# Softmax over 4096 rows: narrow loads of 512 columns in the first tile, and loops that begin at the second tile

## Chip, cores and metric

The kernel runs on one core of a Trainium2 chip. The metric is the device time of one execution in microseconds (us). Runs of the kernel before took 2485.54, 2485.56 and 2485.92 us; the median is 2485.56.

## What is computed

A softmax with a temperature over the last axis of 16 x 256 x 32768 float32 numbers:

```python
scaled = logits / temperature          # temperature = 1.0
scaled = scaled - scaled.max(axis=-1, keepdims=True)
exp_scaled = np.exp(scaled)
return exp_scaled / exp_scaled.sum(axis=-1, keepdims=True)
```

The input has 537 MB and the output as much. Each number is read from memory once and written once.

## The kernel before

A row of 32768 numbers is cut into two halves of 16384, and each half lies on one partition. A tile is 128 such halves, that is 64 rows, so there are 64 tiles (`G`), each 8.4 MB. The array `X` in on-chip memory has three slots (`_BUFS`) of one tile each; tile g uses slot g mod 3. A tile is loaded into its slot, worked on in place, and stored from there.

All transfers are issued by SyncE (SP), in an order written out by `order` (L93) and carried out at L296: loads of tiles 0, 1, 2, store 0, load 3, stores 1 and 2, then load i and store i - 1 by turns, and at the end loads 62 and 63 and stores 61, 62, 63. Each is one instruction with a row of 64 KB per partition, with these exceptions (`load_parts` L68, `store_parts` L76):

- Tile 0's load is one wide load of the first 15360 columns (L151), and then the last 1024 columns (`_NARROW`) in 19 narrow loads (L149). Each narrow load takes 2 to 14 rows that lie 9 apart; the groups come from `narrow_rows` (L82), largest first. Together they cover the 128 rows once.
- Tile 3's load and tile 0's store are in two halves, and the last store is in three parts.

Ahead of a load SP waits until the slot's last store has landed (L144), and ahead of a store until VectorE and ScalarE have scaled the tile (L159, L163).

VectorE and ScalarE work on one tile after another, in pieces of 6304, 5376 and 4704 columns (six pieces in the last two tiles). VectorE waits for the load (`landed`, L198) and takes each piece's negated maximum (L215). ScalarE turns each piece into exponentials and their sum (L275). VectorE swaps the sums and maxima between the two halves of a row (L233) and works out the factors (L237 to L260, with a small exponential on ScalarE, L286). At last VectorE scales two pieces (L266) and ScalarE the first (L294). Neither touches the order of the transfers: they only raise the semaphores that SP waits for.

The instructions of VectorE and ScalarE are written out for the first four tiles (`_HEAD`) and the last three (`_TAIL`); the 57 tiles between are a loop of 19 turns with three tiles each (L307). In the loop the awaited semaphore values are registers that count the turns; a looped tile raises one semaphore per engine and slot when it is scaled, in place of one per piece (L192). `landed` waits for a part of a load ahead of the first piece that needs it: in tile 0 piece 2 alone needs the narrow loads, in tile 3 piece 0 needs the first half, piece 1 both.

At the end SP waits for all stores (L301).

Of the kernel before, what the change touches and what calls it, by code (L numbers as in the profile page):

```python
# [9 lines left out]
_BUFS = 3  # L10
_PLAIN = ((6304, 5376, 4704), (0,))
_LATE = ((4096, 3072, 3072, 2048, 2048, 2048), (3, 4, 5))
_LAST_STORES = ((0, 4096), (4096, 6144), (10240, 6144))
_NARROW = 1024
_NARROW_ROWS = (
    (13, 2), (12, 3), (14,), (11, 3), (10, 4), (9, 5), (8, 6), (7, 7), (4, 4, 3, 3),
)
_HEAD = 4
_TAIL = 3


# [46 lines left out]
def load_parts(g):  # L68
    if g == 0:
        return [(0, _W - _NARROW), (_W - _NARROW, _NARROW)]  # L70
    if g == 3:
        return [(0, _W // 2), (_W // 2, _W // 2)]
    return [(0, _W)]


def store_parts(g, n):  # L76
    if g == 0:
        return [(0, _W // 2), (_W // 2, _W // 2)]
    return list(_LAST_STORES) if g == n - 1 else [(0, _W)]


def narrow_rows(p):  # L82
    step = len(_NARROW_ROWS)
    rows = []
    for q, counts in enumerate(_NARROW_ROWS):
        for n in counts:
            rows.append(slice(q, q + (n - 1) * step + 1, step))
            q += n * step
    assert sum(map(sum, _NARROW_ROWS)) == p
    return sorted(rows, key=lambda r: r.start - r.stop)  # L90


def order(n):  # L93
    plan = [("L", 0), ("L", 1), ("L", 2), ("S", 0), ("L", 3), ("S", 1), ("S", 2)]
    for i in range(4, n - 2):
        plan += [("L", i), ("S", i - 1)]
    return plan + [("L", n - 2), ("L", n - 1), ("S", n - 3), ("S", n - 2), ("S", n - 1)]


@with_exitstack  # L100
def kernel(
# [6 lines left out]
    nc = tc.nc  # L108
    inv_t = 1.0 / float(temperature)
    P = nc.NUM_PARTITIONS  # L110
# [8 lines left out]
    x = xf.rearrange("n (h v) -> (n h) v", h=2)  # L119
    o = of.rearrange("n (h v) -> (n h) v", h=2)  # L120
    G = N * 2 // P
# [6 lines left out]
    X = nc.alloc_sbuf_tensor("xs", [P, _BUFS * _W], fp32)  # L128
# [2 lines left out]
    J = [nc.alloc_sbuf_tensor(f"junk{q}", [P, 2 * most], fp32) for q in range(_BUFS)]  # L131
    R = [nc.alloc_sbuf_tensor(f"row{q}", [P, 4], fp32) for q in range(_BUFS)]
    sig = Signals(nc)
    stored = {}

    def load(g):
        p = Place(g, G)
        rows = slice(g * P, (g + 1) * P)
        for j, (s, n) in enumerate(load_parts(g)):
            if g >= _BUFS:  # L140
                parts = store_parts(g - _BUFS, G)
                for i, (a, m) in enumerate(parts):
                    if a < s + n and s < a + m:
                        nc.sync.wait_ge(*stored[g - _BUFS][i])  # L144
            where = slice(p.slot * _W + s, p.slot * _W + s + n)
            key = ("ld", j, *p.key)
            if g == 0 and j == 1:
                for some in narrow_rows(P):
                    sig.dma(key, nc.sync.dma_start(out=X[some, where], in_=x[some, s : s + n]))  # L149
            else:  # L150
                sig.dma(key, nc.sync.dma_start(out=X[:, where], in_=x[rows, s : s + n]))  # L151

    def store(g):
        p = Place(g, G)
        rows = slice(g * P, (g + 1) * P)
        stored[g] = []
        for i, (s, n) in enumerate(store_parts(g, G)):
            if p.looped:
                nc.sync.wait_ge(sig[("scaled", *p.key)], 2 * p.n)  # L159
            else:  # L160
                for group in (p.own, p.on_act):
                    for k in [k for k in group if k in p.over(s, n)][-1:]:
                        nc.sync.wait_ge(sig[("scaled", k, *p.key)], p.n)  # L163
            where = slice(p.slot * _W + s, p.slot * _W + s + n)
            stored[g].append(
                sig.dma(
                    ("st", i, p.slot),
                    nc.sync.dma_start(out=o[rows, s : s + n], in_=X[:, where]),  # L168
                )
            )  # L170

    class Work:

# [24 lines left out]
        def landed(self, engine, k, seen):  # L198
            s, n = self.p.pieces[k]
            for j, (a, m) in enumerate(load_parts(self.p.g)):  # L200
                if a < s + n and s < a + m and j not in seen:
                    seen.add(j)
                    times = len(narrow_rows(P)) if self.p.g == 0 and j == 1 else 1
                    value = self.p.n16
                    if self.p.g == 3 and j == 1:
                        value, times = 16 * len(narrow_rows(P)) + 16, 1
                    engine.wait_ge(sig[("ld", j, *self.p.key)], value * times)

        def vector(self):
            t, e, r, tv, f, K = self.t, self.e, self.r, self.tv, self.j, self.K  # L210
# [82 lines left out]
                xs = self.piece(k)  # L293
                self.scaled(a.mul(out=xs, in_=xs, mul=f[:, k : k + 1]), k, self.p.on_act)  # L294

    for what, g in order(G):  # L296
        if what == "L":
            load(g)
        else:
            store(g)  # L300
    for key in [key for key in sig.made if key[0] == "st"]:  # L301
        nc.sync.wait_ge(sig[key], sig.made[key])

    for engine, part in ((nc.vector, Work.vector), (nc.scalar, Work.scalar)):
        for g in range(_HEAD):
            part(Work(Place(g, G)))
        with engine.Fori(1, 1 + turns) as turn:  # L307
            turn16 = engine.snap(turn * 16) if engine is nc.vector else None
            for j in range(_BUFS):
                part(Work(Place(_HEAD + j, G, turn, turn16)))  # L310
        for g in range(G - _TAIL, G):
            part(Work(Place(g, G)))

# [34 lines left out]
```

## Time and profile before

| what | value |
|---|---|
| median of the runs | 2485.56 us |
| the profiled execution | 2485.45 us |
| its span, first to last instruction | 2483.7 us |
| moved by DMA, mean rate | 1073.78 MB, 432 GB/s |
| median time from issue to landing, loads / stores of a whole tile | 48.0 / 29.1 us |
| idle time of VectorE that ended with a load's landing | 617.4 us in 60 waits |
| idle time of ScalarE that ended with a maximum (L215) | 1045.6 us in 64 waits |

The chain that ended last, by share of the span: DMA 61%, VectorE 28%, ScalarE 7%.

The page divides the span into 40 slices. A digit is the busy share of a slice in tenths. The chain of waits is followed back from the last instruction, at each step to what released it. A tile passes through the DMA engines about every 38.6 us, load and store together: the loads of successive looped tiles release VectorE at 200.60, 239.69 and 278.77 us at first, and at 2366.22 and 2404.92 us at the end. The trace also keeps every DMA packet with its start, its duration and its size, 17024 of them with data. A row of a transfer is one packet; each transfer ends with semaphore writes of 4 bytes, which the page counts as packets under 512 B (2240).

### The profile page before, as it was taken

The page shows a single profiled execution, that of the slowest core. Times are in us where ns is not written, and L with a number is a line of the kernel's source. Part 1 is how long each engine was busy: PE and PEld are TensorE (multiplying, and loading weights), DVE is VectorE, ACT ScalarE, POOL GpSimd, SP SyncE. Part 2 cuts the span into 40 slices and gives each one's busy share as a digit, 9 for nine tenths or more (in the row PEclk, how much of TensorE's full clock was granted, in tenths as well). Part 3 has the DMA queues.
Part 4 walks back from the last instruction along what each step waited for, and adds up shares of the span by engine and source line. Part 5 has one row for each costly group of instructions (what it writes and reads, how often), then busy time and mean ns, then how long its engine had stood idle before and what let it go on. Part 6 is the DMA issues. An engine that isn't in the chain of part 4 may idle for free.

```text
span 2483.7 us, 1689 instructions
## 1 busy us (share of the span) xinstructions
DVE 1526.0 (61%) x776; ACT 1325.6 (53%) x529; POOL 0.2 (0%) x4
## 2 busy tenths in 40 slices
DVE  5845665666656656566565665656656666566665
ACT  4744645646546455464554645546455464554654
POOL 0000000000000000000000000000000000000000
DMA  9999999999999999999999999999999999999998
GB/s 409 432 437 431 432 437 434 434 433 437 433 432 437 434 434 434 435 434 433 436 434 434 434 435 435 433 435 435 432 435 435 436 432 435 436 432 435 435 436 387
DMA packets 19267, 1073.78 MB, mean 432 GB/s; under 512 B 2240, under 2 KB 2240, under 8 KB 2368
## 3 DMA queue, kind: packets, MB, share of 16 engines
q1 hardware_dynamic: 19264, 1073.75, 99.9%
q14 instruction: 3, 0.02, 0.0%
HBM read 536.87 MB, written 536.87 MB: 432 GB/s over the span
## 4 chain that ended last, share of the span: by engine, by line
DMA 61%; DVE 28%; ACT 7%; issue 2%; SPq 0%; DVEq 0%
DMA xs<-in_logits_dram 59%; DVE t L215 21%; ACT xs L275 6%; DVE xs L266 6%; DMA out_dram<-xs 3%; SPq L168 0%; ACT ee L286 0%; DVE junk L260 0%; DVE t L233 0%; DVE row L257 0%; ACT xs L294 0%; DVE row L237 0%; DVE junk L244 0%; DVEq L307 0%; DVEq L231 0%
## 5 line engine op out<-in xcount | busy, mean ns | idle before, releaser
L275 ACT ACTIVATE xs<-xs,t 128x6304 f32<-128x6304 f32 (+5 forms) x198 | 932.0, 4707 | 1052.5 <-DVE t L215 1045.6
L215 DVE TENSOR_REDUCE t<-xs 128x1 f32<-128x6304 f32 (+5 forms) x198 | 1110.0, 5662 | 617.4 <-DMA xs<-in_logits_dram 617.4
L294 ACT ACTIVATE xs<-xs,junk 128x6304 f32<-128x6304 f32 (+1 forms) x68 | 355.6, 5235 | 44.9 <-DVE junk L260 44.9
L266 DVE TENSOR_SCALAR xs<-xs,junk 128x5376 f32<-128x5376 f32 (+2 forms) x130 | 358.7, 2802 | 2.3
L233 DVE LOAD_MASK_SELECT t<-t x64 | 0.9, 14 | 282.8 <-ACT xs L275 282.8
L286 ACT ACTIVATE ee<-t,row 128x6 f32<-128x6 f32 (+1 forms) x64 | 19.2, 300 | 35.2 <-DVE row L237 35.2
L275 ACT ACTIVATION_READ_ACCUMULATOR xs<-xs,t 128x1 f32 x198 | 36.9, 186 | 0.0
L244 DVE CUSTOM_DVE_ANT_1 junk<-ee,t 128x6 f32<-128x6 f32 (+1 forms) x64 | 10.7, 166 | 23.5 <-ACT ee L286 23.5
L260 DVE TENSOR_SCALAR junk<-ee,row 128x3 f32<-128x3 f32 (+1 forms) x64 | 14.6, 228 | 2.2
L257 DVE RECIPROCAL row<-row 128x1 f32<-128x1 f32 x64 | 10.5, 163 | 2.2
L237 DVE TENSOR_REDUCE row<-t 128x1 f32<-128x6 f32 (+1 forms) x64 | 10.2, 159 | 2.2
L233 DVE STREAM_SHUFFLE t<-t 128x6 f32<-128x6 f32 (+1 forms) x64 | 10.4, 163 | 0.5
L244 DVE DVE_READ_ACCUMULATOR2_ANT row<- 128x1 f32 x64 | 5.3, 82 | 0.0
L275 ACT ACT_TABLE_LOAD x1 | 1.3, 1283 | 0.9 <-SPq L127 0.9
L329 POOL MEMSET const-bfloat16-1.0<- 128x1 bf16 x1 | 0.1, 101 | 0.0
L329 POOL MEMSET const-uint8-127<- 128x1 uint8 x1 | 0.1, 101 | 0.0
L329 POOL MEMSET const-float32-0.0<- 128x1 f32 x1 | 0.1, 98 | 0.2 <-issue 0.2
L329 POOL MEMSET const-float32-1.0<- 128x1 f32 x1 | 0.1, 98 | 0.0
## 6 DMA issues: line engine op xcount, KB each, us to landing
out_dram<-xs SPq DMA_DIRECT2D x2, 4096.0 KB, 28.0
xs<-in_logits_dram SPq DMA_DIRECT2D x2, 4096.0 KB, 19.3
xs<-in_logits_dram SPq DMA_DIRECT2D x1, 7680.0 KB, 21.1
out_dram<-xs SPq DMA_DIRECT2D x2, 3072.0 KB, 19.4
out_dram<-xs SPq DMA_DIRECT2D x1, 2048.0 KB, 12.2
xs<-in_logits_dram SPq DMA_DIRECT2D x62, 48.0
out_dram<-xs SPq DMA_DIRECT2D x62, 29.1
xs<-in_logits_dram SPq DMA_DIRECT2D x4, 12.0 KB
```

What stands on the lines that cost most here:

```text
L215: m = v.tensor_reduce(out=t[:, k : k + 1], in_=self.piece(k), axis=mybir.AxisListType.X, op=A.max, negate=True,)
L233: v.stream_shuffle(out=t[:, 2 * K : 4 * K], in_=t[:, 0 : 2 * K], mask=swap), "sh"
L237: v.tensor_reduce(out=r[:, 0:1], in_=tv[:, :, 0, :], axis=mybir.AxisListType.XY, op=A.min),
L244: v.tensor_tensor_reduce(out=f[:, 0 : 2 * K].rearrange("p (a k) -> p a k", a=2), in0=self.ev, in1=tv[:, :, 1, :], scale=1.0, scalar=0.0, o ...
L257: self.done(v.reciprocal(out=r[:, 2:3], in_=r[:, 1:2]), "rc")
L260: v.tensor_scalar_mul(out=f[:, 0:K], in0=e[:, 0:K], scalar1=r[:, 2:3]), "f"
L266: v.tensor_scalar_mul(out=xs, in0=xs, scalar1=f[:, k : k + 1]), k, self.p.own
L275: s = a.activation(out=xs, in_=xs, func=Exp, bias=t[:, k : k + 1], scale=inv_t, accum_out=t[:, K + k : K + k + 1],)
L286: a.activation(out=self.ev, in_=self.tv[:, :, 0, :], func=Exp, bias=r[:, 0:1], scale=-1.0),
L294: self.scaled(a.mul(out=xs, in_=xs, mul=f[:, k : k + 1]), k, self.p.on_act)
L329: nc = _bacc.Bacc("TRN2", target_bir_lowering=False, num_devices=1)
```

## The change

Two constants change: the narrow loads take the last 512 columns of tile 0 and the wide load the first 15872, with the same 19 groups of rows; and the instructions of VectorE and ScalarE are written out for tile 0 alone, after which a loop of 20 turns covers tiles 1 to 60. The rest of the diff makes the semaphores fit the loop: the parts of a load share one semaphore (the narrow loads have their own), and VectorE waits for the whole load of a tile ahead of its first piece, in tile 3 for both halves; tile 0 keeps its two waits. For that each turn has two counted register values in place of one. The list `order` is replaced by loops that issue the same transfers in the same order. At the end SP waits for 16 instead of 32 on the semaphore that the second part of the last store shares with that of tile 0's.

The diff, without the part that spells out the order and the tuple of SP's store:

```diff
-_NARROW = 1024
+_NARROW = 512
...
-_HEAD = 4
+_HEAD = 1
...
+def stored(g, n):
+    parts = len(store_parts(g, n))
+    return [(("st", i, g % _BUFS), 16 * (g // _BUFS + 1 if i == 0 else 1)) for i in range(parts)]
...
             if g >= _BUFS:
-                parts = store_parts(g - _BUFS, G)
-                for i, (a, m) in enumerate(parts):
+                parts = zip(store_parts(g - _BUFS, G), stored(g - _BUFS, G))
+                for (a, m), (which, value) in parts:
                     if a < s + n and s < a + m:
-                        nc.sync.wait_ge(*stored[g - _BUFS][i])
+                        nc.sync.wait_ge(sig[which], value)
             where = slice(p.slot * _W + s, p.slot * _W + s + n)
-            key = ("ld", j, *p.key)
             if g == 0 and j == 1:
                 for some in narrow_rows(P):
-                    sig.dma(key, nc.sync.dma_start(out=X[some, where], in_=x[some, s : s + n]))
+                    sig.dma(
+                        ("narrow",), nc.sync.dma_start(out=X[some, where], in_=x[some, s : s + n])
+                    )
             else:
-                sig.dma(key, nc.sync.dma_start(out=X[:, where], in_=x[rows, s : s + n]))
+                sig.dma(
+                    ("ld", *p.key), nc.sync.dma_start(out=X[:, where], in_=x[rows, s : s + n])
+                )
...
             for j, (a, m) in enumerate(load_parts(self.p.g)):
-                if a < s + n and s < a + m and j not in seen:
+                if self.p.g == 0 and a < s + n and s < a + m and j not in seen:
                     seen.add(j)
-                    times = len(narrow_rows(P)) if self.p.g == 0 and j == 1 else 1
-                    value = self.p.n16
-                    if self.p.g == 3 and j == 1:
-                        value, times = 16 * len(narrow_rows(P)) + 16, 1
-                    engine.wait_ge(sig[("ld", j, *self.p.key)], value * times)
+                    if j == 0:
+                        engine.wait_ge(sig[("ld", *self.p.key)], 16)
+                    else:
+                        engine.wait_ge(sig[("narrow",)], 16 * len(narrow_rows(P)))
+            if self.p.g > 0 and k == 0:
+                engine.wait_ge(sig[("ld", *self.p.key)], self.p.n16)
...
         for g in range(_HEAD):
             part(Work(Place(g, G)))
         with engine.Fori(1, 1 + turns) as turn:
-            turn16 = engine.snap(turn * 16) if engine is nc.vector else None
+            count16 = [None, None]
+            if engine is nc.vector:
+                count16 = [engine.snap((turn + k) * 16) for k in range(2)]
             for j in range(_BUFS):
-                part(Work(Place(_HEAD + j, G, turn, turn16)))
+                g = _HEAD + j
+                part(Work(Place(g, G, turn, count16[g // _BUFS])))
```

More of the change, by code (lines that the diff above doesn't have):

```diff
@@ L90, in narrow_rows @@
     return sorted(rows, key=lambda r: r.start - r.stop)
[L93 to L97, printed above, removed]
+def stored(g, n):
+    parts = len(store_parts(g, n))
+    return [(("st", i, g % _BUFS), 16 * (g // _BUFS + 1 if i == 0 else 1)) for i in range(parts)]
 @with_exitstack
@@ L133, with load @@
     sig = Signals(nc)
-    stored = {}
-    def load(g):
-        p = Place(g, G)
+    def load(p):
+        g = p.g
         rows = slice(g * P, (g + 1) * P)
@@ L140, in load, with store @@
             if g >= _BUFS:
-                parts = store_parts(g - _BUFS, G)
-                for i, (a, m) in enumerate(parts):
+                parts = zip(store_parts(g - _BUFS, G), stored(g - _BUFS, G))
+                for (a, m), (which, value) in parts:
                     if a < s + n and s < a + m:
-                        nc.sync.wait_ge(*stored[g - _BUFS][i])
+                        nc.sync.wait_ge(sig[which], value)
             where = slice(p.slot * _W + s, p.slot * _W + s + n)
-            key = ("ld", j, *p.key)
             if g == 0 and j == 1:
                 for some in narrow_rows(P):
-                    sig.dma(key, nc.sync.dma_start(out=X[some, where], in_=x[some, s : s + n]))
-            else:
-                sig.dma(key, nc.sync.dma_start(out=X[:, where], in_=x[rows, s : s + n]))
-    def store(g):
-        p = Place(g, G)
+                    sig.dma(
+                        ("narrow",), nc.sync.dma_start(out=X[some, where], in_=x[some, s : s + n])
+                    )
+            else:
+                sig.dma(
+                    ("ld", *p.key), nc.sync.dma_start(out=X[:, where], in_=x[rows, s : s + n])
+                )
+    def store(p):
+        g = p.g
         rows = slice(g * P, (g + 1) * P)
-        stored[g] = []
         for i, (s, n) in enumerate(store_parts(g, G)):
@@ L164, in store @@
             where = slice(p.slot * _W + s, p.slot * _W + s + n)
[L165 to L170, printed above, removed]
+            sig.dma(("st", i, p.slot), nc.sync.dma_start(out=o[rows, s : s + n], in_=X[:, where]))
     class Work:
@@ L294, in scalar @@
                 self.scaled(a.mul(out=xs, in_=xs, mul=f[:, k : k + 1]), k, self.p.on_act)
[L296 to L302, printed above, removed]
+    for g in range(_BUFS):
+        load(Place(g, G))
+    store(Place(0, G))
+    load(Place(_BUFS, G))
+    for g in (1, 2):
+        store(Place(g, G))
+    for g in range(_BUFS + 1, G):
+        load(Place(g, G))
+        if g < G - 2:
+            store(Place(g - 1, G))
+    for g in range(G - _TAIL, G):
+        store(Place(g, G))
+    counts = {}
+    for g in range(G):
+        for which, value in stored(g, G):
+            counts[which] = value
+    for which, value in counts.items():
+        nc.sync.wait_ge(sig[which], value)
     for engine, part in ((nc.vector, Work.vector), (nc.scalar, Work.scalar)):
```

## The prediction

> **What bounds the kernel now.** I read first the page's slices and its list of DMA queues, then the busy time by windows, then the chain of waits, and last the single DMA packets that the trace keeps.
>
> ```profile
> DVE 1526.0 (61%) x776; ACT 1325.6 (53%) x529; POOL 0.2 (0%) x4
> ...
> DMA  9999999999999999999999999999999999999998
> ...
> q1 hardware_dynamic: 19264, 1073.75, 99.9%
> ```
>
> The 16 DMA engines are busy in every slice; the compute engines are not. Now the windows (columns: stretch, its length, busy us of DVE, ACT and POOL, clock, DMA share, GB/s):
>
> ```profile
> 1.50:4.50 3.00, 0.00 (x0) 0.69 (x1) 0.00 (x0) 1.00 0.99 328
> 4.50:20.50 16.00, 0.00 (x0) 0.00 (x0) 0.00 (x0) 1.00 1.00 430
> 20.50:28.00 7.50, 5.90 (x1) 0.00 (x0) 0.00 (x0) 1.00 1.12 393
> ...
> 140.00:300.00 160.00, 88.85 (x39) 76.36 (x29) 0.00 (x0) 1.00 1.00 432
> 300.00:2400.00 2100.00, 1293.77 (x657) 1122.21 (x436) 0.00 (x0) 1.00 1.00 434
> ...
> 2476.00:2484.00 8.00, 0.00 (x0) 0.00 (x0) 0.00 (x0) 1.00 0.25 108
> ```
>
> The reader is to see three losses against 434 GB/s: the first packets, the stretch 20.5 to 28 us in which the narrow loads run, and the last 8 us, in which only some engines still work.
>
> The packets explain these. On one DMA engine the next packet starts 3 to 4 ns before the last one's recorded end, so all packets can be strung into 16 chains. From tile 1 on the chains have no hole but three of 302 ns (at 187.5, 268.4 and 931.9 us). A packet of 65536 B takes 2418 ns (median; 32768 B takes 1213, 16384 B 611), and a chain moves one tile in 8 of them. So an engine's end is the sum of its own packets, and the kernel ends with the slowest engine. The narrow loads put an unequal number of rows on the engines: the chains show 0 to 19 narrow packets, 8 on average. Five chains (us from the first instruction; the last column is the last packet of tile 1's load):
>
> ```
> narrow packets  wide load ends  tile 1 begins  its first packet, ns  tile 1 ends
>       0             21.21          21.21              3434              41.97
>       5             21.16          22.05              3733              42.70
>      11             21.01          23.28              3313              43.52
>      14             21.34          24.56              2840              44.32
>      19             20.91          25.17              2616              44.72
> ```
>
> Sixteen engines finish tile 1 spread over 2.76 us, and the last store spread over 5.16 us: the last packet ends at 2481.96, the first engine's last at 2476.80. The engine that ends last is not one with 19 narrow packets. It is one that finished tile 1 at 43.52 us, 1.55 us behind the first engine, with 11 of them, and that then falls back some 20 ns in each of the 130 DMAs that follow (about 2.4 us), plus 0.08 and 0.37 us in disturbed packets around 158 and 235 us and 0.75 us at 932 us, where one 302 ns hole and a packet of 2835 ns fall on it. The others end at 2480.8 or before.
>
> **The change part by part.** All sums are for that last engine, against the profiled execution's own 2485.45 us (span 2483.7, 1.75 around it), which is 0.11 below the median of 2485.56.
>
> *Wide load, 15360 to 15872 columns:* its 8 packets grow by 2048 B each. Between 61440 B (2267 ns) and 65536 B (2418 ns) a byte costs 0.0369 ns, so 75.5 ns a packet: **+0.60 us** on all engines alike.
>
> *Narrow loads, 4096 to 2048 B a packet:* no packet of 2048 B with data is in the trace. The nearest row, 4096 B, takes 159 ns undisturbed and 287 at most; the slope above gives 84 undisturbed. On the engine of interest 11 of them with their semaphore writes took 23.28 - 21.01 = 2.27 us, 207 ns each. Lower end: undisturbed, 88 ns each with the write, 0.97 us. Upper end: the price does not fall at all, 2.27 us. I take the same disturbance in proportion, 207 x 84/159 = 109 ns, 1.20 us: **-1.07 us** (0 to -1.30).
>
> *The disturbance of tile 1:* its first packet took 3313 ns on this engine, 895 over 2418, while the other engines still read narrow rows. That phase gets half as long, so I take half, **-0.45 us** (0 to -0.90).
>
> *Issue of the narrow loads:* still 19 instructions, and they are covered:
>
> ```profile
> 1.38 13.88 SPq L149 DMA_DIRECT2D xs<-in_logits_dram  x19
> 15.31 0.89 SPq L151 DMA_DIRECT2D xs<-in_logits_dram  x2
> 22.10 17.34 DVE L215 TENSOR_REDUCE t<-xs 128x1 f32<-128x6304 f32 x3 [22.10 <-DMA xs<-in_logits_dram]
> ```
>
> SP has issued tile 2's load at 16.2 us, 4.7 us before the first engine ends the wide load (20.89). The third row starts 0.60 us later, and with it tile 0's store (50.84). That is hidden: the first engine has tiles 1 and 2 to load until 61.3 us.
>
> *Tile 3's merged wait:* VectorE waited for the halves of tile 3's load separately and now waits for both ahead of the first piece. Behind that wait stand tile 3's reductions, then ScalarE's exponentials and SP's store. Both halves are in at 102.8 us by the packets and VectorE reaches tile 3 at 107.96 after tile 2, so it costs nothing; without these 5.1 us of cover it could cost the 9.7 us between the halves.
>
> *Loop from tile 1:* three tiles' code goes from VectorE and ScalarE, one more turn comes:
>
> ```profile
> L307 DVEq FUSED_REGOPS  x19: 44/44/44, 131.1 to 2235.2; - x19
> L307 DVEq ALU_OP  x19: 40/40/52, 263.0 to 2350.8; - x19
> L307 DVEq COMPARE_BRANCH  x19: 50/56/69, 263.0 to 2350.9; - x19
> ```
>
> A turn costs VectorE 0.14 us, and one register operation more, perhaps 0.2. At tile 1 VectorE has no idle time to hide it in, but tile 1's store waits until 84.35 us behind tile 3's second load, while its data are ready at 79.3; and tile 2's store, issued at 108.4, has engines with work until 119.4. Cost nothing; a stall would have to pass 11 us to leave an engine dry. SP's list of transfers and its order stay; a looped tile's store waits on one semaphore's total in place of two pieces' own, for the same instructions. The dropped final wait for the second part of the last store lies ahead of the third part on each engine: nothing.
>
> *The holes:* 302 ns is what 8192 B take at the rate above, and code goes; whether a hole leaves the last engine I can't tell: 0 to -0.75, I take 0, since the 932 us hole falls where VectorE and ScalarE repeat their loop.
>
> Sum: 0.60 - 1.07 - 0.45 = **-0.9 us**, 2484.5 against this execution, 2484.6 against the median. The engines with 19 packets gain 0.60 - 2.0 - 0.1 = -1.5 and stay behind it in rank.
>
> **Rivals.** *Flat packets:* a narrow packet's price in this crowd may be per packet and not per byte (246 ns at the 75th percentile against 159). Then narrow loads keep their 2.27 us and the wide load's 0.60 is added: 2486.1. The Trainium skill, "DMA: Bandwidth & Descriptors", section Bandwidth, says that transfers under 64 KB are dominated by their descriptors, which leans this way; the undisturbed 159 ns, in line with 1213 and 2418, do not.
>
> *Re-spread:* disturbed packets at 158 and 235 us cost this engine 0.45 us; they depend on how the phases fall and could give the gain back: about 2485.4.
>
> *Luck:* the 932 us hole falls on another engine, or the disturbed packets stay away: another 0.45 to 0.75 less, about 2484.0 to 2483.4.
>
> *Phases too close (slower):* the engines would leave tile 1 spread over about 1.4 us in place of 2.76. If closeness made them meet in memory at each tile, the stretch at 140 to 300 us shows the price: 432 in place of 434 GB/s over 2100 us is 9.7 us, 2494. The Trainium skill, same page, section Latency and other measured facts, tells of rows a large power of two apart that halve the rate, and suspects streams in lock-step. It speaks against this change; rows here lie 64 KiB apart. Against it: in the wide load all engines run within 0.62 us of each other, and their packets settle at the floor of 2267 ns after the first one's 2959 (mean). It decides only where the spread falls below these 0.62 us, or for loads beside stores, which no row shows that close.
>
> *Stall at the loop (slower):* over 11 us at tile 1 or 2, each us more being one us: 2486 and up. At the later turns up to 10 us of it would be hidden under VectorE's wait for loads, so the trace does not exclude it. The Trainium skill, "Runtime: NRT & Kernel Launch", section Instruction fetch mechanics, says that a taken branch out of the window stalls for a fetch; no row shows one of this size.
>
> **How the numbers follow.** Forecast (2484.1 to 2485.1) 0.51; re-spread 0.18; luck 0.13; flat packets 0.11; phases 0.05; stall 0.01; something over 5 us faster 0.01. Two in a thousand of this kernel is 5.0 us, about what a measurement can tell from no change; all but the last three cases lie within it: faster 0.01, same 0.93, slower 0.06. The range goes from luck with the lower ends, 2483.2, to flat packets with half a us of disturbed ones, 2486.6.
>
> **What would show it.** Narrow packets of 84 to 150 ns; the engine with 11 ending tile 1 near 42.6 us; the spread after tile 1 under 2 us; packets of 2418 ns from 300 us on; the last 8 us moving more than 108 GB/s. A hole in a chain before 300 us, or 65536 B packets with a median over 2422 ns, would prove me wrong.

## The result, and the profile after

The changed kernel took 2503.84 us in the median of 20 runs (2485.57 to 2510.36); the kernel before 2485.9 (2485.08 to 2486.27, 20 runs). The ratio is 1.0052, with a 95% interval of 1.0036 to 1.0067: it is slower. The forecast was 2484.6 us, with a range of 2483.2 to 2486.6.

The times of the changed kernel form two groups: 8 of the 20 between 2485.6 and 2486.9 us, 12 between 2498.8 and 2510.4, with nothing between. The granted clock is 1.000 in both, and the kernel before, timed in turn with it on the same chip, has one group only; so the changed kernel itself has two ways to run. Below they are called the lower and the upper group. The profiled execution fell in the lower one (2485.87 us, span 2484.1). Its windows, with the columns as before:

```profile
1.50:4.50 3.00, 0.00 (x0) 0.69 (x1) 0.00 (x0) 1.00 1.03 339
4.50:20.50 16.00, 0.00 (x0) 0.00 (x0) 0.00 (x0) 1.00 1.03 444
20.50:28.00 7.50, 5.56 (x1) 0.00 (x0) 0.00 (x0) 1.00 1.06 402
...
140.00:300.00 160.00, 89.20 (x42) 77.01 (x31) 0.00 (x0) 1.00 1.00 432
300.00:2400.00 2100.00, 1293.61 (x654) 1121.56 (x434) 0.00 (x0) 1.00 1.00 434
...
2476.00:2484.10 8.10, 0.00 (x0) 0.00 (x0) 0.00 (x0) 1.00 0.27 115
```

The reader is to see that this execution is the old one with a slightly better stretch of narrow loads (402 in place of 393 GB/s) and a slightly fuller end (115 in place of 108); the 444 is a matter of counting, since a packet counts where it begins and the wide ones are longer. It tells nothing of the 20 us in the median. The upper group shows in a later profile of the same kernel (e4, 2509.48 us, span 2507.7):

```profile
60.00:300.00 240.00, 151.23 (x76) 136.50 (x54) 0.00 (x0) 1.00 1.00 433
300.00:900.00 600.00, 364.06 (x188) 315.83 (x122) 0.00 (x0) 1.00 1.00 434
900.00:1500.00 600.00, 367.96 (x182) 313.55 (x121) 0.00 (x0) 1.00 1.00 427
1500.00:2100.00 600.00, 365.60 (x190) 321.57 (x128) 0.00 (x0) 1.00 1.00 429
```

For 900 us it runs like the other, at 434 GB/s. Then it drops to 427 to 429 GB/s and stays there, with the DMA share still at 1.00: the engines look busy but some of their packets take longer. From 1000 to 2400 us 7.9% of the packets of 65536 B take over 2440 ns and their mean is 2448.5; in the profile of the lower group it is 0.1% and 2418.3. The median is 2418 in both.

What happens at 900 us shows when the finish of each transfer is read engine by engine. The lag is the time from the first of the 16 engines that ends a transfer to the last (from the semaphore writes in the packet records, us):

```
ends at about    42    235    467    699    931   1165   2340 us
before          2.76   3.62   3.95   3.97   3.98   3.98   4.90
after, lower    2.27   2.66   3.79   4.55   4.71   4.71   5.54
after, upper    2.54   3.32   5.36   6.61   8.71   9.18   8.14
e3              0.70   2.60   4.47   5.62   6.72   8.60   8.62
g1              2.98   3.07   3.89   2.72   3.13   3.18   2.99
g2              2.54   3.31   5.00   5.55   5.55   5.55   7.84
g4              2.28   2.23   2.20   2.19   2.19   2.17   2.15
```

In the upper group five or six engines fall back ("creep"): the lag grows by over 0.1 us per transfer until it is near 8.7 us. There the chains of the leading engines get holes of up to 0.6 us, on many at once; in e4 the first are at 911 us. The timeline of e4 shows one such place, and the windows around it what the DMA engines begin there (by the same counting):

```profile
968.62 0.33 SPq L164 DMA_DIRECT2D out_dram<-xs  x1
968.99 0.43 SPq L150 DMA_DIRECT2D xs<-in_logits_dram  x1
978.84 17.34 DVE L210 TENSOR_REDUCE t<-xs 128x1 f32<-128x6304 f32 x3 [10.25 <-DMA xs<-in_logits_dram]
```

```profile
968.40:968.90 0.50, 0.19 (x1) 0.14 (x1) 0.00 (x0) 1.00 0.60 262
968.90:969.40 0.50, 0.00 (x0) 0.00 (x0) 0.00 (x0) 1.00 0.00 0
969.40:969.90 0.50, 0.00 (x0) 0.00 (x0) 0.00 (x0) 1.00 3.38 1442
```

SP issues a store at 968.62 us. The load queued ahead of it lands, on the last engine, at 978.8; the leading engines ended their share about 9 us earlier and have nothing until the store reaches them, about 1 us after its issue. Then they all begin a packet within 0.5 us of one another. These packets are hardly slow: they take 2418 to 2478 ns. The slow ones of this tile are two others: the last packet of the load on the six engines that trail (2545 to 2938 ns), and the last packet of the store on the ten that lead (3161 to 3521 ns, begun at 986.5 to 986.8 us).

### The profile page after: what moved, and what is told of

Its sections match the earlier page's. It is cut to its first block, busy times and chain, and to the rows that moved or that the text cites. A ratio compares the mean times of both kernels' runs of the same rounds, so it can differ in the third digit from the quotient of the medians.

```text
span 2484.1 us, 1715 instructions
## 1 busy us (share of the span) xinstructions
DVE 1526.3 (61%) x776; ACT 1325.6 (53%) x529; POOL 0.2 (0%) x4
## 4 chain that ended last, share of the span: by engine, by line
DMA 61%; DVE 27%; ACT 7%; issue 3%; SPq 0%; DVEq 0%
DMA xs<-in_logits_dram 59%; DVE t L210 21%; ACT xs L270 6%; DVE xs L261 5%; DMA out_dram<-xs 3%; SPq L164 0%; ACT ee L281 0%; DVE junk L255 0%; DVE t L228 0%; DVE row L252 0%; ACT xs L289 0%; DVE row L232 0%; DVE junk L239 0%; DVEq L313 0%; DVEq L226 0%
## 5 line engine op out<-in xcount | busy, mean ns | idle before, releaser
L232 DVE TENSOR_REDUCE row<-t 128x1 f32<-128x6 f32 (+1 forms) x64 | 10.2, 159 | 2.2
```

What stands on the lines that cost most here:

```text
L232: v.tensor_reduce(out=r[:, 0:1], in_=tv[:, :, 0, :], axis=mybir.AxisListType.XY, op=A.min),
```

## The experiments

All times are medians with the lowest and highest; the kernel before stands at 2485.7 to 2486.0 in each set. "Upper" counts times above 2495 us. Two counts in the texts written ahead are off by one: of the changed kernel's first 20 times 8 and 12 lie in the two groups, not 9 and 11, and at 512 columns 24 of 38 were upper, not 23.

**Which part does it.** e1 has the narrow loads alone, e2 the loops alone.

```diff
 # e1: the kernel before
-_NARROW = 1024
+_NARROW = 512
 # e2: the changed kernel
-_NARROW = 512
+_NARROW = 1024
```

> The kernel before with narrow loads of 512 columns; the loops still begin at the fifth tile. The changed kernel's times fall in two groups, 9 of 20 at 2485.6 to 2486.9 us and 11 of 20 at 2498.8 to 2510.4. Theory A (phases: the 16 DMA engines leave the first tile's load less far apart, and some executions then fall into a persistent meeting of their packets): both groups appear here too, about half of the times at 2498 to 2510. Theory B (loop: an occasional stall when VectorE and ScalarE enter the loop at the second tile leaves the DMA engines dry): all times at 2484.5 to 2486.5, one group. Theory C (the merged wait of tile 3, or both edits together): one group as well.

> The changed kernel with narrow loads of 1024 columns again; the loops begin at the second tile. Theory A (phases): one group, 2485 to 2486.5 us, as before. Theory B (loop): two groups as in the changed kernel, half of the times 13 to 25 us up. Theory C: two groups if the merged wait does it, one if both edits are needed.

e1: 2506.17 us (2486.51 to 2510.28), 5 of 6 upper, ratio 1.0068 (1.0043 to 1.0093). e2: 2485.88 us (2485.50 to 2486.61), none of 11 upper, ratio 1.0000 (0.9991 to 1.0009). The narrow loads make the whole difference; the loop, the merged wait and the final wait cost nothing. Theories B and C fall.

**Without narrow loads, and the changed kernel again.**

```diff
 # e3: the kernel before
 def load_parts(g):
-    if g == 0:
-        return [(0, _W - _NARROW), (_W - _NARROW, _NARROW)]
...
-                        value, times = 16 * len(narrow_rows(P)) + 16, 1
+                        value, times = 16, 1
```

> The kernel before without narrow loads: tile 0 comes in one load of 16384 columns, so that nothing sets the DMA engines apart. Theory A (phases): the slow group in most or all times, 2498 to 2515 us, and if the profiled execution falls in it, packets of 65536 B with a mean well over 2420 ns from 300 us on. Theory B and C: one group near 2483 to 2485 us, since no engine has more bytes than another and the disturbed stretch at 20.5 to 28 us goes.

> The changed kernel again, unedited, for the share of its slow times and, if the profiled execution falls in that group, for where its 13 to 25 us are lost. Theory A: spread over the whole run, the mean GB/s of 300 to 2400 us at 430 to 432 in place of 434, no hole in a chain of packets over 1 us. Theory B: one hole of 13 to 25 us in all 16 chains before 300 us, and 434 GB/s after it.

e3: 2504.34 us (2484.72 to 2506.18), 5 of 7 upper. e4: 2505.09 us (2485.36 to 2511.87), 7 of 12 upper. Theory A holds in both, with one correction: the loss is not spread over the whole run, it begins at some point between 900 and 1100 us, when the lag has grown.

Where the creep is made can be read from the packets. It is the eighth and last packet of a load, on engines that end the load over 0.5 us after the first one (late engines). Its mean excess over 2418 ns, by stretch:

```
                     240 to 900 us   1000 to 2400 us
e4 (upper)                241              466
e3 (upper)                217              396
e1 (upper)                194              479
after (lower)             110                4
h2 (lower)                114                5
e2 (1024 columns)          76               14
before                      2                3
h3 (2048 columns)           0                0
```

In these executions the last packets of stores have next to none from 240 to 900 us (0 to 2 ns). From 1000 us on those of the leading engines, within 0.5 us of the first, have 379 ns in e4 and 372 in e1, and none in the profile of the lower group. So an execution of the lower group creeps too, but there the creep ends before the lag reaches 7 us. The narrow loads of 1024 columns do not rule it out: e2 has it, and in the kernel before the same packets of late engines have 36 ns on average when the stretch is taken from 60 us on.

**What turns the lag into time.** g1 lengthens the work between a load's landing and the tile's store, which VectorE's idle time covers; g2 shortens it.

```diff
 # g1: the kernel before
                 self.landed(v, k, seen)
+                if k == 1 and self.p.looped:
+                    v.tensor_reduce(
+                        out=r[:, 3:4], in_=self.piece(k), axis=mybir.AxisListType.X, op=A.max
+                    )
 # g2: the changed kernel
-                    in_=self.piece(k),
+                    in_=self.piece(k)[:, 0 : self.p.pieces[k][1] // 8],
```

> The kernel before with VectorE taking the maximum of piece 1 twice in each looped tile (5.65 us more between a load's landing and the tile's store), which its 10 us of idle time per tile would hide. In the slow executions of e1, e3 and e4 five engines fall back until they are some 8.7 us behind the others; from there the leading engines show holes at every few tiles and a tile takes 39.2 us in place of 38.6. Theory run-dry: 8.7 us is how long the leading engines' work lasts when a store is issued, since a store cannot be issued before the last engine has landed the load and 29 us of compute have passed. Then 5.65 us more compute bring the point down to about 3.0 us, which the kernel before passes at 160 to 200 us (lag 3.1 to 3.5): every execution at 2500 to 2520 us, with holes from 200 us on. Theory creep alone (the late engines' own slow packets are the whole loss, holes are a side effect): 2485 to 2487 us, as the idle time covers the added instruction.

> The changed kernel with the maximum taken over the first eighth of each piece only (the exponentials use that bound in place of the true maximum). The store follows the landing about 6 us sooner, so the leading engines' work lasts about 15 us. Theory run-dry: no holes until a lag of about 15 us, so the slow executions lose only the late engines' creep (100 to 150 ns per transfer, lag at the end up to 15 us in place of 8.6): slow group at 2490 to 2498 us, fast group at 2485 to 2487. Theory creep alone: slow group unchanged at 2498 to 2510.

g1: 2518.79 us (2516.70 to 2520.11), ratio 1.0135 (1.0119 to 1.0150), all of 4 upper, with the narrow loads of the kernel before. Its holes begin at 196.7 us, where the lag passes 3.1 to 3.5 us, and its rate is low from the first windows on (g1, same columns):

```profile
60.00:300.00 240.00, 170.99 (x78) 129.54 (x51) 0.00 (x0) 1.00 1.00 429
300.00:900.00 600.00, 447.99 (x204) 319.14 (x126) 0.00 (x0) 1.00 1.00 428
```

VectorE is busy for 448 of 600 us there and in the whole run still waits 324.5 us for loads, so it is not the bound. A tile takes 39.18 us, as in e4, though the lag is 3 us in place of 9. g2: 2488.08 us (2487.52 to 2489.03), none of 11 upper, no hole in any chain but three single ones of 302 or 309 ns, and 434 GB/s to the end although the lag reaches 7.84 us at 2340 us (8.1 at the end):

```profile
900.00:1500.00 600.00, 139.44 (x190) 325.15 (x128) 0.00 (x0) 1.00 1.00 434
1500.00:2100.00 600.00, 136.86 (x184) 308.92 (x122) 0.00 (x0) 1.00 1.00 435
```

So the point moves with the compute chain in the way run-dry says. How it makes packets slow is another matter: the holes themselves are short, and no run shows why the last packets take longer from there on. What g2 did not show is its upper group of 2490 to 2498 us: the creep stopped at 5.55 us in all engines but one.

**What protects the kernel before.** g3 has as many narrow bytes, evenly laid.

```diff
 # g3: the kernel before; 8 narrow packets on each engine
-_NARROW_ROWS = (
-    (13, 2), (12, 3), (14,), (11, 3), (10, 4), (9, 5), (8, 6), (7, 7), (4, 4, 3, 3),
-)
+_NARROW_ROWS = ((16,),) * 8
```

> The kernel before with narrow loads of 1024 columns in 8 groups of 16 rows in place of 19 uneven ones: the same bytes, the same narrow packets, but 8 on every engine, so that they leave the engines together. Theory spread (what protects the kernel before is that the engines leave tile 0 some 4 us apart): two groups, half or more of the times at 2500 to 2510 us, as without narrow loads. Theory packets (the narrow packets themselves or their time matter, not how unevenly they lie): one group at 2484 to 2486.5.

g3: 2502.91 us (2501.86 to 2505.70), all of 5 upper. It is how the narrow packets lie on the engines, not their bytes or their number, that keeps the kernel before in the lower group. (g3 also issues 8 narrow loads in place of 19; h1 below issues 16 and stays in the lower group.)

**Does the creep need the stores?**

```diff
 # g4: the changed kernel
-            sig.dma(("st", i, p.slot), nc.sync.dma_start(out=o[rows, s : s + n], in_=X[:, where]))
+            if p.looped:
+                sig.dma(("st", i, p.slot), nc.sync.dma_start(out=X[:, where], in_=x[rows, s : s + n]))
+            else:
+                sig.dma(("st", i, p.slot), nc.sync.dma_start(out=o[rows, s : s + n], in_=X[:, where]))
```

> The changed kernel with each looped tile's store replaced by a second load of the same tile into its slot: the same bytes, order and waits, but no writes to memory between tiles 1 and 60, whose outputs stay unwritten. In e1, e3 and e4 the creep is made almost wholly by one packet: the last of eight in a load (about 250 ns more on average, on engines that finish a load over 0.5 us after the first one), and never by the last of a store. Theory mix (the other engines' stores beside that packet disturb it): no creep, one group at 2484 to 2486 us. Theory place (it lies in the last packet of any load with a transfer queued behind it): creep at twice the rate, most times at 2500 us or more.

g4: 2486.22 us (2485.99 to 2486.63), none of 11 upper. The lag stays at 2.2 us for the whole run, and the last packets of late engines have an excess of 2.9 ns. The time is just above the range that theory mix gave, and a packet of 65536 B takes 2422 ns in the median in place of 2418. Loads beside loads do not creep; theory mix holds, theory place falls.

**How much spread is needed, and of what shape.**

```diff
 # h1: the kernel before; 16 packets on engines 0 to 7, none on the others
+_NARROW_ROWS = ((8,),) * 16
 # h2
+_NARROW = 768
 # h3
+_NARROW = 2048
```

> The kernel before with its narrow loads of 1024 columns in 16 groups of 8 rows: engines 0 to 7 get 16 narrow packets each, the others none, so that the engines leave tile 0 as two bunches some 3 us apart, with hardly any spread inside a bunch. Theory spread (how far the last engine is from the first is what protects): one group at 2485 to 2487 us, as in the kernel before. Theory bunch (it is eight or more engines finishing loads within half a us, while others are late, that starts the creep): two groups or all slow, 2498 to 2520 us; the late bunch has eight engines, so the lag may pass 8.7 us sooner than 900 us.

> The kernel before with narrow loads of 768 columns, half way between the two sizes, so the engines leave tile 1 some 2.5 us apart. Both theories of the creep: between the share of slow times at 512 columns (23 of 38 in all) and at 1024 (none), so some 0 to 50 percent at 2498 to 2510 us, the others at 2485 to 2487.

> The kernel before with narrow loads of 2048 columns: the engines leave tile 1 some 6 us apart. No slow group by either theory of the creep; the engines with 19 narrow packets carry 2 to 3 us more, so 2487 to 2489 us. If a spread of 6 us and some 2.5 us of slow falling back brings the lag to 8.7 us before the end, the run-dry theory expects holes from there and up to 2495 us.

h1: 2488.48 us (2488.11 to 2490.72), none of 11 upper: theory bunch falls and theory spread fits for the group, though not for the time, which is some 3 us behind the kernel before. h2: 2486.29 us (2485.34 to 2506.91), 2 of 12 upper. h3: 2487.06 us (2486.88 to 2487.45), none of 11 upper, its lag going from 5.57 to 6.2 us. With uneven groups the share of upper times goes 24 of 38 at 512 columns, 2 of 12 at 768, none at 1024 (e2 and all runs of the kernel before) and 2048; with the engines close together (e3, g3, 0.7 us apart after tile 1) it is 10 of 12. The spread after tile 1 does not sort single executions: the profiled ones at 2.19 us (h2) and 2.27 (the changed kernel) fell in the lower group, those at 2.49 (e1) and 2.54 (e4) in the upper.

**The shorter chain where every time was upper.** The edit is g2's, made to g3.

> The kernel of g3 (1024 narrow columns in even groups, all five times at 2501.9 to 2505.7 us) with the maximum taken over the first eighth of each piece only, as in g2, so that a store follows its load some 6 us sooner and the leading engines' work lasts about 15 us. Theory run-dry: no holes before a lag of 15 us; what is left is the creep of the late engines: one group or two between 2487 and 2498 us, the spread at the end 6 to 15 us. Theory creep alone: 2500 to 2506 us as in g3, the spread at the end over 15 us. If the lag stops near 5 to 8 us as in g2 and the time is 2486 to 2489, the shorter chain also weakens the creep, which run-dry by itself does not explain.

i1: 2487.36 us (2486.28 to 2488.24), none of 11 upper; the lag grows to 4.2 us and no further. The last case of the text came, with a lag below the 5 to 8 us it named: a shorter chain avoids the running dry and also weakens the creep. There the disturbed packets fall on the early engines too (101 ns on average, against 195 on the late ones), so nobody is left behind.

No version beat the kernel before clearly; e2 equals it.

## Why the prediction was wrong

- **The step that failed** is the price of the packets after tile 1. The prediction carried over the falling back of the trace of before, "some 20 ns in each of the 130 DMAs that follow (about 2.4 us)", and expected "packets of 2418 ns from 300 us on". So it put at nothing what a smaller spread does to every later tile; only a rival at 0.05 had it. What came: on the engines over 3 us behind, e4's last packet of a load took 235 ns more from 240 to 900 us and 479 ns more from 1000 to 2400 us. For the 39 tiles from about 936 us on e4 takes 39.18 us a tile where the lower group takes 38.64, which is 21 of the 23.6 us between the two spans, and on the trailing engines the 479 ns are most of the 0.54 us a tile.
- **"An engine's end is the sum of its own packets, and the kernel ends with the slowest engine"** still holds for the trailing engines: in e4 none that is over 3 us behind has a hole between a load and the store after it. It misses that the engines are tied. A store waits for the last engine's share of the load and 29 us of compute; at its issue the last engine has some 10 us of the next load left, and a leading one has less, by as much as it is ahead. With a lag of 8 to 9 us the leading engines run dry. Their holes are small, 1.3 us per engine on average in the whole run; most of what they lose is in the last packets of stores (379 ns each).
- **The sign that was named could not show it.** A median over 2422 ns was to prove the prediction wrong, and the median is 2418 in every upper profile: the loss sits in 8% of the packets.
- **The rival "phases too close"** was the right one, with a chance of 0.05. Its mechanism was right in kind: closeness, "for loads beside stores, which no row shows that close". Its point was wrong: it was put at 0.62 us of spread, but the executions of e1 and e4 that left tile 1 2.5 us apart fell into it, and none profiled with 2.6 us or more did but g1, whose chain is longer. So was its form: the packets do not meet at each tile from the start; a slow creep feeds a lag that costs little until the leading engines run dry. Its price of 9.7 us is 22 (medians of the groups 2486.24 and 2508.28 over 32 times).
- **The sum of the terms** was about right where it was tested. The narrow packets took 99 ns on average (84 to 192; 109 taken). The first wide share ended 0.55 us later (0.60). Tile 1's packets gained 41 ns each, 0.33 us (0.45). But the spread after tile 1 fell to 2.27 us only, not 1.4, and the lower group gained nothing: its median is 0.3 us above the kernel before. The 110 ns of creep on late engines are enough to take the gain back (17 loads from 240 to 900 us, 1.9 us), which is the rival "re-spread" in kind, though later than the 158 and 235 us that it named.
- **The loop terms** were right. e2 holds the loop at the second tile, the merged wait and the dropped final wait at no cost. The Trainium skill, "Runtime: NRT & Kernel Launch", section Instruction fetch mechanics, has a taken branch stall for a fetch when its target lies outside the fetched window; by e2 nothing of that reaches the end here. The single holes of 302 ns are instruction fetches: the trace of before has three instruction packets of 8192 B, and they end at 187.50, 268.38 and 931.88 us, where the holes end.
- **"Flat packets", "luck" and "stall"** did not come: the narrow packets took 99 ns and not the 206 of before, no time was below 2485.36 us in 32, and e2 shows no stall.
- The profile could have warned: VectorE's wait ahead of each load was 10.2 us, and that is how long the last engine's queue lasts after a store's issue; the leading engines' lasts shorter by the lag. A lag of 5.2 us against 10 us of queue was half of a margin, and the prediction priced the lag as an end effect only.

What stays open: why it is the last packet of a transfer that is disturbed, why executions of one kernel differ in whether the creep ends in time, why a shorter compute chain weakens it, and whether and how the running dry makes last packets slower. That the creep needs the other engines' stores is shown by g4; the memory effect behind it is not. That the layout of the narrow loads and the length of the chain decide the share of upper times is shown by e1, e2, g1 and g3; the step from holes to slow packets is not, since the holes themselves are too short for the loss. i1 and g3 were timed on different chips, and the unedited changed kernel was not timed on the chip of g2, so those two comparisons assume that the chips are alike; the kernel before is (2485.7 to 2486.0 us on the three).

## What to carry to other kernels

When a transfer is shared by 16 engines and its consumer waits for all of them, compare the engines' lag with the time that the queue behind it lasts: compute that is hidden under idle time still uses up that queue (g1: 5.65 us of "free" VectorE work in each looped tile cost 33 us in all). A small, odd-looking edit that sets the engines apart may be what holds a bandwidth-bound kernel together. A median duration can hide a loss that sits in one packet of sixteen. And one profile, or three runs, cannot show a kernel that has two ways to run: the profiled execution after was within 0.5 us of the one before.

## What the runs showed of the hardware

- The last packet of a load on an engine that trails the others took some 195 to 240 ns more on average from 240 to 900 us and 396 to 479 ns more from 1000 to 2400 us (e1, e3, e4), and 2.9 ns where the others do not write to memory (g4). The last packet of a store took no more up to 900 us; later it took 372 to 379 ns more on the leading engines of e1 and e4.
- Starting in step costs little by itself: e3's engines leave tile 1 0.70 us apart and its loads run like the others' (2422.5 ns a packet of 65536 B from 300 to 900 us, against 2423.7 in e4), and the ten packets that begin together at 969.5 us in e4 take 2418 to 2478 ns. The Trainium skill, "DMA: Bandwidth & Descriptors", section Latency and other measured facts, gives halved rates for rows a large power of two apart and infers streams in lock-step. The rows lie 64 KiB apart here in every run, so no run shows what that distance does; the rate was 434 GB/s in the lower group and 427 to 429 in the upper.
- How 128 narrow packets of 84 to 287 ns lie on the engines in the first 26 us changes how often the other 2460 us take the slow way: in 24 of 38 times with 512 uneven columns, in none with 1024 uneven ones, in 5 of 5 with 1024 laid evenly (g3).
